# Rotated queries and keys written to DRAM by heads, in four pieces, in a two-layer hybrid decoder step

## Chip, cores and metric

The kernel runs on one core of one Trainium2 chip. The metric is the time on the device in microseconds (us), the median over several runs of one kernel. The engines are named as in the profile: PE (TensorE, matmul; PEld is its weight load), DVE (VectorE), ACT (ScalarE), POOL (GpSimd) and SP (SyncE, which here only issues DMAs). ACT issues DMAs too: the weights. The queues of SP and ACT end on the same 16 DMA engines of the core.

## What is computed

One inference step of a two-layer trunk: a prompt of 1024 positions and eight single-token samples with caches. Each layer projects its input once, runs attention on one half of the columns and an RWKV-7 recurrence on the other, and ends in a feed-forward network:

```
q, k = rope(q, pos), rope(k, pos)              # 8 heads x 64
att  = sum over patterns (128,1),(512,4),(2048,16) of softmax attention, merged by denominators
rw   = rwkv7_time_mix(token_shift(p[rwkv columns]))
x1   = layer_norm(alpha*x + concat(rms_norm(att)*gain, rw) @ w_out)
y    = layer_norm(alpha*x1 + relu(x1 @ w_ff_up)^2 @ w_ff_down)
```

The rotated keys and the values are outputs as well.

## The kernel before

**Tiling.** Activations lie transposed, 128 columns of the model on the partitions and positions along the row. The prompt is cut into two halves `h` of 512 positions (the second carries the eight sample tokens along). Every dense product is three matmuls (a high and a low part of the activation with the high part of the weight, the high part of the activation with the low part of the weight): lines 370 to 372. ACT makes the high part of a weight tile (line 343) and DVE the low part (line 344); there are four tiles of each, so PE can work on weights that were made some time before, and no further.

**Order.** PE's order is written by a planner, `Streams`: six generators (projection and feed-forward, RWKV stage 1 and 2, attention, the values' transposes, the cached keys) are interleaved by estimated times, and the result is fixed. The instructions of ACT, DVE, POOL and the DMA issues of SP are put in order at build time by a scheduler with a time model. All engines run their list in order.

**Queries and keys.** In `in_proj`, for each layer `l`, half `h` and pair of heads `p` (16 combinations), PE makes q, k and v of two heads. The columns of the weight are ordered so that a tile `t` of q or k has its 128 partitions as (f, d, r): f is the half of the rotation (2), d the head (2), r the index in it (32). `rope` (lines 657 to 664) rotates `t` with two DVE and two POOL instructions, and one DMA on SP's queue writes its 128 rows of 2 KB to `d_qkv` in DRAM (line 638). The keys go to the output too (line 640).

**Loads for the attention.** `att_load` (lines 1488 to 1531) reads them back by head. `heads` views the 128 rows as (f, d, r), so a head is two blocks of 32 rows that lie 64 rows apart. `stage` loads a head's 64 rows twice, into the upper and the lower half of a tile `stg` (line 1500, a pair of DMAs), of which there are two buffers. From each staged tile ACT makes `qS` or `kS` (lines 1522 and 1526) and POOL the low part `qL` or the low half of `kS` (lines 1523 and 1527); then the buffer is free. The first half stages q and k of two heads (four pairs), the second also the last 128 keys of the first half (six pairs), and loads `qf` and `kf` for the distant keys in two DMAs each, one per head (lines 1514 and 1515). Most loads begin at the end of the attention before (`ahead`, line 1482).

What the attention needs from this is `qS`, `qL`, `kS` for the scores `pS` (lines 1565 and 1566) and `qf`, `kf` for line 1554.

Of the kernel before, what the change touches and what calls it, by code (L numbers as in the profile page):

```python
# [28 lines left out]
HB = T // 2  # L29
# [115 lines left out]
class Streams:  # L145
# [24 lines left out]
    def note(self, *key):  # L170
        self.times[key] = self.now

    def after(self, *key, lat=0):
        return lambda: self.times[key] + lat if key in self.times else None
# [73 lines left out]
def body(ctx, tc, I, O):  # L248
    nc = tc.nc
    PE, V, A, G, S = nc.tensor, nc.vector, nc.scalar, nc.gpsimd, nc.sync  # L250
# [22 lines left out]
    def C(name):  # L273
        a, n = CAT[name]
        return cst[:, a:a + n]
# [24 lines left out]
    def both(f):  # L300
        return [[f(l, h) for h in range(2)] for l in range(DEPTH)]
# [5 lines left out]
    d_qkv = both(lambda l, h: dr.tile([4, 3, 128, HB], F32, name=f"d_qkv{l}{h}"))  # L307
# [71 lines left out]
    def dense(items, kts, xhh, xll, evac):  # L379

        res = []
        yield (0, None, 0, "d")
        yield from dense_steps(items, kts, xhh, xll, res)
        for it, p in zip(items, res):
            r = evac(it, p)
            if r is not None:
                yield r
        for i, it in enumerate(items):
            yield (res[-1] if i == 0 else 0, ("d", 900 + 500 * i), 0, None)
# [8 lines left out]
    def proj_order():  # L398
        seq = [("z", 0)]
        for p in range(4):  # L400
            if p < 3:
                seq.append(("z", p + 1))
            seq.append(("a", p))
        return seq
# [147 lines left out]
    def in_proj(l, h, hook=None, tail=None, then=None):  # L552
# [27 lines left out]
        def z_ev(p, j):  # L580
            def put(c0, n, d):
                S.dma_start(d_z[l][h][p, j, :, c0:c0 + n], d[:, :n])
            return shifted(l, h, muv(4 * j + p), 128, 4 * j + p, put)
# [30 lines left out]
        for kind, p in proj_order()[1:]:  # L614
            if kind == "a" and p == 3 and then is not None:
                yield from then()
            for j in range(3):
                w = W.take()
                if kind == "z":
                    ev = z_ev(p, j)  # L620
                    for c0, n in ck:
                        yield from dense([(w, 128, c0, n)], K8, xhc, xlc, ev)
                    continue
                seq = (2 * l + h) * 4 + p
                if j == 1 and seq > 0:
                    yield after("post", seq - 1)
                t = ap_.tile([128, HN[1]], F32, tag="qe", bufs=2, name="qe")

                def eva(it, pt):
                    _, _, c0, n = it  # L630
                    (V.tensor_copy if c0 else A.copy)(t[:, c0:c0 + n], pt[:, :n])
                for c0, n in CK[h]:
                    yield from dense([(w, 128, c0, n)], K8, xhc, xlc, eva)
                if j == 0 and h == 1:
                    t8 = ap_.tile([128, 5, 8], F32, tag="t8", name="t8")
                if j < 2:
                    rope(t, HN[h], tabs)
                    S.dma_start(d_qkv[l][h][p, j], t[:, 0:HB])
                    if j == 1:
                        S.dma_start(O["k_p"][l, p, :, h * HB:h * HB + HB], t[:, 0:HB])  # L640
                if h == 1 and j == 0:
                    if p == 0:
                        sq[l] = (rq.tile([128, 4, 32], F32, tag="q2", name="q2"), rq.tile([128, 4, 8], F32, tag="kn", name="kn"))
                        G.memset(sq[l][0], 0.0)
                    G.memset(t8[:, 1:4, :], 0.0)
                    for hd in range(2):
                        G.tensor_scalar(sq[l][0][:, p, hd:16:2], t[:, HB:HN[1]], C("hm")[:, hd:hd + 1], None, op0=ALU.mult)
                elif h == 1:
                    G.tensor_scalar(t8[:, (0, 4)[j - 1], :], t[:, HB:HN[1]], 1.0, None, op0=ALU.mult)
                    if j == 1:  # L650
                        G.tensor_scalar(sq[l][1][:, p, :], t[:, HB:HN[1]], 1.0, None, op0=ALU.mult)
            if kind == "a":
                qe[seq] = (l, h, p, t, t8 if h == 1 else None)
                note("qe", seq)
            note(kind, l, h, p)

    def rope(t, n, tabs):

        m = ap_.tile([128, HN[1]], F32, tag="rt", name="rm")
        for x in range(2):  # L660
            a, b = slice(64 * x, 64 * x + 64), slice(64 - 64 * x, 128 - 64 * x)
            V.tensor_tensor(m[a, :n], t[b, :n], tabs[b, 1, :n], op=ALU.mult)
        G.tensor_tensor(t[:, :n], t[:, :n], tabs[:, 0, :n], op=ALU.mult)
        G.tensor_tensor(t[:, :n], t[:, :n], m[:, :n], op=ALU.add)
# [179 lines left out]
    def half(l, h, prev=None):  # L844
# [169 lines left out]
        if not last:  # L1014
            store(*cl[0])
            note("proj", l + 1, h)

            def hook(i):
                if i == 0:
                    yield from ln.finish(*cl[1], spread=1)  # L1020
                ln.scale(SPI[i], evs[-1])
                if i == 5:
                    store(*cl[1])

            def tail():
                if h == 1:
                    S.dma_start(O["shift"][l + 1].rearrange("k p t -> p k t"), t[:, :, HB - 1:HN[1]])
            yield from in_proj(l + 1, h, hook, tail, mix_load(l + h, 1 - h))
        elif h == 0:
            def beside(o):  # L1030

                if o == 0:
                    yield from mixes_late[0].norm()
                if o == 1:
                    yield from ln.finish(*cl[1], spread=1)
                if o >= 1:
                    ln.scale(SPY[o], evs[-1])
            mixes_late = [mixes[l, 1]]
            yield from half(l, 1, beside)
        else:  # L1040
            yield from ln.finish(*cl[1])
# [16 lines left out]
    def dense_stream():  # L1058
        t = x_fetch(0)
        load_par()  # L1060
        x_load(0, t)
        t = x_fetch(1)
        yield from in_proj(0, 0, lambda i: init() if i == 1 else None)
        x_load(1, t)
        yield from in_proj(0, 1, then=mix_load(0, 0))
        for l, h in ((0, 0), (0, 1), (1, 0)):
            yield from half(l, h)
# [420 lines left out]
    def att_load(l, h, p):  # L1488

        qS, qL, kS = [], [], []

        def heads(src):
            return src.rearrange("(f d r) t -> d f r t", f=2, d=2)

        def stage(src, hd, n):
            t = ap_.tile([128, HB], F32, tag="stg", bufs=2, name="stg")[:, :n]
            for x in range(2):
                S.dma_start(t[64 * x:64 * x + 64], heads(src)[hd])  # L1500
            return t

        def byres(t):
            return t.rearrange("p (j a c) -> p j c a", a=32, c=4)

        def inrow(t):
            return t.rearrange("p (j c a) -> p j c a", a=32, c=4)

        qf = kf = None
        if h == 1:  # L1510
            qf, kf = (ap_.tile([128, HB], F32, tag=x, name=x) for x in ("qf", "kf"))
            for hd in range(2):
                hs = slice(64 * hd, 64 * hd + 64)
                S.dma_start(qf[hs], heads(d_qkv[l][1][p, 0])[hd])
                S.dma_start(kf[hs], heads(d_qkv[l][0][p, 1])[hd])
        for hd in range(2):
            hs, ls = slice(64 * hd, 64 * hd + 64), slice(64 - 64 * hd, 128 - 64 * hd)
            q = ap_.tile([128, HB], F32R, tag=f"q{hd}", name="qS")
            ql = ap_.tile([128, HB], F32R, tag=f"ql{hd}", name="qL")
            k = ap_.tile([128, HB + 128], F32R, tag=f"k{hd}", name="kS")  # L1520
            t = stage(d_qkv[l][h][p, 0], hd, HB)
            A.copy(inrow(q), byres(t))
            AQ.tensor_tensor(inrow(ql), byres(t), inrow(q.bitcast(F32)), op=ALU.subtract)
            for src, c, n in [(d_qkv[l][0][p, 1][:, HB - 128:HB], 0, 128)] * h + [(d_qkv[l][h][p, 1], 128 * h, HB)]:
                t = stage(src, hd, n)
                A.copy(k[:, c:c + n], t)
                AQ.tensor_tensor(k[ls, c:c + n], t[ls], k.bitcast(F32)[ls, c:c + n], op=ALU.subtract)
            qS.append(q)
            qL.append(ql)
            kS.append(k)  # L1530
        return qS, kS, qL, qf, kf, R.now + 6000 + 1000 * (h + 1)
# [328 lines left out]
```

## Time and profile before

| | us |
|---|---|
| median of three runs | 3555.35 |
| lowest and highest run | 3549.26, 3558.99 |
| the profiled execution, its own time | 3560.94 |
| its span, first to last instruction | 3559.1 |
| PE busy | 3202.7 |
| PE weight load busy | 2697.6 |
| DVE busy | 2055.5 |
| ACT busy | 1448.3 |
| POOL busy | 979.3 |

The profile shows one execution. Busy times are shares of the span; a wait is put down to what ended it. The mean granted clock of TensorE over the span is 0.949 of full speed. DMAs are issued in order on a queue; the time from issue to landing is told by who waited for the data.

### The profile page before, as it was taken

The page shows a single profiled execution, that of the slowest core. Times are in us where ns is not written, and L with a number is a line of the kernel's source. Part 1 is how long each engine was busy: PE and PEld are TensorE (multiplying, and loading weights), DVE is VectorE, ACT ScalarE, POOL GpSimd, SP SyncE. Part 2 cuts the span into 40 slices and gives each one's busy share as a digit, 9 for nine tenths or more (in the row PEclk, how much of TensorE's full clock was granted, in tenths as well). Part 3 has the DMA queues.
Part 4 walks back from the last instruction along what each step waited for, and adds up shares of the span by engine and source line. Part 5 has one row for each costly group of instructions (what it writes and reads, how often), then busy time and mean ns, then how long its engine had stood idle before and what let it go on. Part 6 is the DMA issues. An engine that isn't in the chain of part 4 may idle for free. (4 is left out here: it accounts for less than half of the span.)

```text
span 3559.1 us, 65853 instructions
## 1 busy us (share of the span) xinstructions
PE 3202.7 (90%) x24732; PEld 2697.6 (76%) x24732; DVE 2055.5 (58%) x4703; ACT 1448.3 (41%) x3266; POOL 979.3 (28%) x1841
## 2 busy tenths in 40 slices
PE   8788897977999998888999999797797999889998
PEld 6567776765777687677899998685675677789998
DVE  4455554764554664567565457465764564685556
ACT  4345333443343344344443336343443333453334
POOL 2324233531111421435211113334412121340012
PEclk9899998988999999998999999898898999999999
DMA  7334343433443335442333235344243343333332
GB/s 219 107 113 124 115 115 103 129 95 99 117 112 85 106 97 163 139 150 68 86 98 92 80 98 154 117 126 133 71 118 100 111 113 91 117 101 91 94 90 84
DMA packets 366533, 393.55 MB, mean 111 GB/s; under 512 B 141848, under 2 KB 219112, under 8 KB 366216
## 3 DMA queue, kind: packets, MB, share of 16 engines
q10 hardware_dynamic: 121152, 213.44, 20.9%
q1 hardware_dynamic: 245064, 175.92, 16.9%
q8 instruction: 195, 3.19, 0.4%
q14 instruction: 122, 1.00, 0.1%
HBM read 325.30 MB, written 63.97 MB: 109 GB/s over the span
## 5 line engine op out<-in xcount | busy, mean ns | idle before, releaser
L370 PE MATMUL dps<-xh,wh 128*128 128x256 f32 (+3 forms) x2984 | 1006.9, 337 | 31.0 <-ACT xh L758 15.0
L371 PE MATMUL dps<-xl,wh 128*128 128x256 f32 (+3 forms) x2984 | 956.8, 321 | 10.4 <-DVE xl L759 8.6
L372 PE MATMUL dps<-xh,wl 128*128 128x256 f32 (+3 forms) x2984 | 953.3, 319 | 1.2 <-DVE wl L344 1.0
L344 DVE TENSOR_TENSOR wl<-wr,wh 128x512 fp32r<-128x512 f32 (+1 forms) x772 | 581.8, 755 | 501.3 <-ACT wh L343 485.6
L343 ACT CAST wh<-wr 128x512 fp32r<-128x512 f32 (+1 forms) x772 | 475.1, 616 | 844.4 <-PE dps L371 777.8
L370 PEld LDWEIGHTS dps<-xh,wh 128*128 128x128 f32 x2984 | 576.6, 193 | 106.4 <-issue 31.0
L371 PEld LDWEIGHTS dps<-xl,wh 128*128 128x128 f32 x2984 | 576.8, 193 | 46.3 <-DVE xl L759 12.5
L372 PEld LDWEIGHTS dps<-xh,wl 128*128 128x128 f32 x2984 | 575.6, 193 | 41.0 <-DVE wl L344 2.6
L370 PE MATMUL dps<-hh,wh 128*128 128x512 f32 (+2 forms) x1600 | 536.1, 335 | 5.4 <-DVE hh L941 3.6
L371 PE MATMUL dps<-hl,wh 128*128 128x512 f32 (+2 forms) x1600 | 513.1, 321 | 4.5 <-DVE hl L830 3.3
L372 PE MATMUL dps<-hh,wl 128*128 128x512 f32 (+2 forms) x1600 | 512.0, 320 | 0.0
L370 PEld LDWEIGHTS dps<-hh,wh 128*128 128x128 f32 x1600 | 303.5, 190 | 45.2 <-issue 17.7
L371 PEld LDWEIGHTS dps<-hl,wh 128*128 128x128 f32 x1600 | 304.1, 190 | 22.6 <-DVE hl L830 4.1
L372 PEld LDWEIGHTS dps<-hh,wl 128*128 128x128 f32 x1600 | 303.9, 190 | 22.6
L1209 POOL TENSOR_TENSOR tm<-BL,XB 32x15 f32<-32x15 f32 (+7 forms) x480 | 153.0, 319 | 496.5 <-DMA BL<-d_el 375.9
L973 DVE TENSOR_TENSOR t<-dps,t 128x256 f32<-128x256 f32 (+1 forms) x240 | 123.6, 515 | 161.1 <-PE dps L372 160.7
L1211 POOL TENSOR_TENSOR XB<-XB,tm 32x15 f32<-32x15 f32 (+7 forms) x480 | 154.6, 322 | 34.4
L726 POOL TENSOR_TENSOR ln<-ln,lsq 128x256 f32<-128x256 f32 (+1 forms) x112 | 91.2, 814 | 232.5 <-ACT lsq L724 229.9
L941 DVE CAST hh<-rl 128x256 fp32r<-128x256 f32 (+2 forms) x200 | 74.4, 372 | 108.6 <-ACT rl L940 105.4
L939 ACT ACTIVATE rl<-dps 128x256 f32<-128x256 f32 (+2 forms) x200 | 88.4, 442 | 102.2 <-PE dps L372 89.9
L715 POOL TENSOR_TENSOR t<-t,ln 128x256 f32<-128x256 f32 (+1 forms) x32 | 28.1, 913 | 352.1 <-ACT ln L709 352.1
L370 PE MATMUL dps<-hh,xh 128*128 128x256 f32 (+1 forms) x368 | 112.6, 306 | 13.3 <-DVE t L1006 7.2
(345 smaller groups left out, 5098.0 us busy)
## 6 DMA issues: line engine op xcount, KB each, us to landing
wr<-in_w_ff_up ACTq DMA_DIRECT2D x272, 256.0 KB
wr<-in_w_ff_down ACTq DMA_DIRECT2D x256, 256.0 KB
wr<-in_w_in ACTq DMA_DIRECT2D x220, 256.0 KB
stg<-d_qkv SPq DMA_DIRECT2D x128, 128.0 KB
wr<-in_w_out ACTq DMA_DIRECT2D x64, 256.0 KB
z<-d_z SPq DMA_DIRECT2D x24, 384.0 KB
d_qkv<-qe SPq DMA_DIRECT2D x32, 256.0 KB
kvc<-in_cache_k SPq DMA_DIRECT2D x32, 256.0 KB
```

Source lines behind the costliest of these rows:

```text
L343: self.copies.append(A.copy(h[:, :, :m], w[:, :, :m]))
L344: V.tensor_tensor(lo[:, :, :m], w[:, :, :m], h.bitcast(F32)[:, :, :m], op=ALU.subtract)
L370: PE.matmul(p[:m, :n], wh[:, wk % 4, :m], hi, start=(i == 0), stop=False)
L371: PE.matmul(p[:m, :n], wh[:, wk % 4, :m], lo, start=False, stop=False)
L372: PE.matmul(p[:m, :n], wl[:, wk % 4, :m], hi, start=False, stop=(i == last))
L715: G.tensor_tensor(t, t, self.cm[:, c0:c0 + n], op=ALU.subtract)
L726: G.tensor_tensor(s2, s2, sq, op=ALU.add)
L939: A.activation(r, p[:, :n], AF.Relu)
L941: V.tensor_copy(hh[:, c0:c0 + n], r)
L973: V.tensor_tensor(to, p[:, :n], to, op=ALU.add)
L1209: G.tensor_tensor(tv, bc(BL[:, 17 * j + 1:17 * j + 2], [(1, m), (0, j + 1)]), bc(XB[:, 16 * j:16 * j + 1], [(0, m), (1, j + 1)]), op=ALU.mult)
L1211: G.tensor_tensor(xv, xv, tv, op=ALU.add)
```

## The change

The four blocks (f, d) of a rotated tile are written by a DMA each, to the place where head d has its 64 rows in one piece. The loads then take 64 rows that lie together, and `qf` and `kf` are one DMA each, both heads at once. Nothing else is changed: the keys' output keeps its layout.

```diff
@@ in_proj
                 if j < 2:
                     rope(t, HN[h], tabs)
-                    S.dma_start(d_qkv[l][h][p, j], t[:, 0:HB])
+                    for f in range(2):
+                        for d in range(2):
+                            a, b = 64 * f + 32 * d, 64 * d + 32 * f
+                            S.dma_start(d_qkv[l][h][p, j, b:b + 32], t[a:a + 32, 0:HB])
@@ att_load
-        def heads(src):
-            return src.rearrange("(f d r) t -> d f r t", f=2, d=2)
-
         def stage(src, hd, n):
             t = ap_.tile([128, HB], F32, tag="stg", bufs=2, name="stg")[:, :n]
             for x in range(2):
-                S.dma_start(t[64 * x:64 * x + 64], heads(src)[hd])
+                S.dma_start(t[64 * x:64 * x + 64], src[64 * hd:64 * hd + 64])
             return t
@@ att_load, second half
-            for hd in range(2):
-                hs = slice(64 * hd, 64 * hd + 64)
-                S.dma_start(qf[hs], heads(d_qkv[l][1][p, 0])[hd])
-                S.dma_start(kf[hs], heads(d_qkv[l][0][p, 1])[hd])
+            S.dma_start(qf, d_qkv[l][1][p, 0])
+            S.dma_start(kf, d_qkv[l][0][p, 1])
```

On PE the order of all instructions stays the same. On ACT, DVE and POOL no instruction is added or removed and some move by a few places. SP has 96 more writes (line 638, 32 become 128) and 16 fewer loads of `qf` and `kf`. Two places on SP's queue follow; line numbers after 641 shift by two or three in the changed kernel.

SP, the first layer's first pair of heads: the key's write, the loads of the first head's key, the second head's query and key (`stg`), and one `kf`. Before:

```order
L638 DMA d_qkv_108<-qe 128x512
L640 DMA out_k_p<-qe 128x512
L1500 DMA stg<-d_qkv_108 64x1x512 x4
L1515 DMA kf<-d_qkv_108 64x1x512
L678 DMA out_v_p<-rt 128x4x128
L680 DMA d_qkv_108<-rt 128x512
L1500 DMA stg<-d_qkv_108 64x1x512 x2
L1515 DMA kf<-d_qkv_108 64x1x512
L1471 DMA vT<-d_qkv_108 128x512
```

The same place in the changed kernel:

```order
L641 DMA d_qkv_108<-qe 32x512 x4
L643 DMA out_k_p<-qe 128x512
L1500 DMA stg<-d_qkv_108 64x512 x4
L681 DMA out_v_p<-rt 128x4x128
L683 DMA d_qkv_108<-rt 128x512
L1513 DMA kf<-d_qkv_108 128x512
L1500 DMA stg<-d_qkv_108 64x512 x2
L1474 DMA vT<-d_qkv_108 128x512
```

The write has become four, the two loads of `kf` one, which stands behind the values' write; the order is otherwise the same.

SP, second layer, second half: the loads for the second pair of heads, with `qf` and `kf`, around the sample tokens' outputs. Before:

```order
L1500 DMA stg<-d_qkv_111 64x1x512 x2
L1514 DMA qf<-d_qkv_111 64x1x512
L1515 DMA kf<-d_qkv_110 64x1x512
L1514 DMA qf<-d_qkv_111 64x1x512
L1515 DMA kf<-d_qkv_110 64x1x512
L1500 DMA stg<-d_qkv_111 64x1x512 x2
L1500 DMA stg<-d_qkv_110 64x1x128 x2
L678 DMA out_v_p<-rt 128x4x128
L680 DMA d_qkv_111<-rt 128x512
```

The same place in the changed kernel:

```order
L1500 DMA stg<-d_qkv_111 64x512 x2
L1512 DMA qf<-d_qkv_111 128x512
L1513 DMA kf<-d_qkv_110 128x512
L1500 DMA stg<-d_qkv_111 64x512 x2
L1500 DMA stg<-d_qkv_110 64x128 x2
L681 DMA out_v_p<-rt 128x4x128
L683 DMA d_qkv_111<-rt 128x512
```

Two DMAs fewer stand here between the first staged tile and the next; nothing else moved.

## Rows read from the trace of the kernel before

**Rows 1.** The page: busy time of PE and ACT, granted clock in 40 slices.
```profile
PE 3202.7 (90%) x24732; PEld 2697.6 (76%) x24732; DVE 2055.5 (58%) x4703; ACT 1448.3 (41%) x3266; POOL 979.3 (28%) x1841
...
PEclk9899998988999999998999999898898999999999
```

**Rows 2.** Busy time by stretch, 15 stretches (us) with loads for the attention.
```profile
core 0: us, PE busy (x) PEld busy (x) DVE busy (x) ACT busy (x) POOL busy (x), PEclk, DMA share, GB/s
70.00:125.00 55.00, 40.65 (x227) 31.72 (x227) 21.21 (x45) 18.23 (x40) 24.04 (x44) 0.88 0.45 134
...
2665.00:2715.00 50.00, 30.40 (x193) 20.77 (x189) 16.80 (x44) 12.29 (x25) 8.42 (x14) 0.76 0.25 76
sum 860.00, PE 599.93 PEld 486.99 DVE 393.15 ACT 313.25 POOL 309.99; mean PE 40.00 PEld 32.47 DVE 26.21 ACT 20.88 POOL 20.67
```

**Rows 3.** The same view, five stretches with attention and RWKV steps, but without such loads.
```profile
190.00:230.00 40.00, 40.00 (x288) 28.97 (x286) 25.54 (x72) 16.53 (x45) 15.29 (x40) 1.00 0.40 115
...
2575.00:2665.00 90.00, 89.43 (x772) 66.78 (x768) 54.98 (x147) 41.85 (x102) 13.59 (x42) 1.00 0.43 122
sum 380.00, PE 376.31 PEld 300.22 DVE 242.48 ACT 167.87 POOL 110.45; mean PE 75.26 PEld 60.04 DVE 48.50 ACT 33.57 POOL 22.09
```

**Rows 4.** Who waited for whom, whole span: us in total, times, longest us.
```profile
DVE wl L344 <- ACT wh L343: 485.6, 309, 17.3
...
ACT kS L1526 <- DMA stg<-d_qkv: 191.7, 33, 16.6
...
ACT qS L1522 <- DMA stg<-d_qkv: 120.7, 19, 15.3
```

**Rows 5.** Instructions in order of time, one load: start, us, what, [idle before <-releaser].
```profile
2393.24 11.96 SPq L1500 DMA_DIRECT2D stg<-d_qkv  x4
...
2396.01 0.60 ACT L343 CAST wh<-wr 128x512 fp32r<-128x512 f32 x1
2397.37 0.33 ACTq L342 DMA_DIRECT2D wr<-in_w_out  x1
2411.87 1.09 ACT L1522 CAST qS<-stg 128x512 fp32r<-128x512 f32 x1 [15.25 <-DMA stg<-d_qkv]
...
2413.68 0.75 ACT L1325 COPY TV<-pPQ 64x256 f32<-64x256 f32 x2
...
2414.10 1.12 PE L1342 MATMUL pO<-LB,TV 128*64 128x128 f32 x8 [14.16 <-ACT TV L1325]
```

**Rows 6.** Busy time by stretch: one in which hardly any other DMA runs beside a stage.
```profile
2553.00:2559.00 6.00, 6.00 (x36) 5.77 (x37) 6.00 (x5) 0.00 (x0) 5.18 (x9) 0.76 0.13 46
```

**Rows 7.** DMA issues: how many, KB each.
```profile
stg<-d_qkv SPq DMA_DIRECT2D x128, 128.0 KB
...
kf<-d_qkv SPq DMA_DIRECT2D x16, 128.0 KB
```

**Rows 8.** The chain that ended last, pieces that end on a stage: start, us, what.
```profile
2241.29 12.67 DMA stg<-d_qkv
...
2396.64 15.15 DMA stg<-d_qkv
...
2698.09 7.96 DMA stg<-d_qkv
```

**Rows 9.** The same chain: other DMAs from issue to landing.
```profile
2236.54 3.04 DMA d_qkv<-qe
...
2855.60 2.18 DMA d_el<-LB
...
2893.37 3.29 DMA ST<-in_state_wkv
```

**Rows 10.** In order of time: the state's load in two halves of 64 partitions, and its user.
```profile
2892.83 1.14 SPq L1656 DMA_DIRECT2D ST<-in_state_wkv  x2
...
2896.78 0.69 DVE L1657 TENSOR_TENSOR dt<-ST,DV 128x512 f32<-128x512 f32 x1 [2.99 <-DMA ST<-in_state_wkv]
```

**Rows 11.** Busy time by stretch: 33 stretches at half clock among those of rows 2.
```profile
88.10:94.90 6.80, 4.92 (x14) 4.05 (x15) 4.22 (x9) 2.12 (x6) 2.77 (x7) 0.50 0.34 114
105.10:108.60 3.50, 2.84 (x9) 2.48 (x10) 1.18 (x4) 0.00 (x0) 2.25 (x7) 0.51 0.63 188
...
sum 290.40, PE 151.15 PEld 125.36 DVE 101.94 ACT 98.21 POOL 99.36; mean PE 4.58 PEld 3.80 DVE 3.09 ACT 2.98 POOL 3.01
```

**Rows 12.** By tile: issues and casts, times each: ns min/median/max, first and last start.
```profile
L1500 SPq DMA_DIRECT2D stg<-d_qkv x160: 482/509/3642, 75.5 to 2698.1; - x160
L638 SPq DMA_DIRECT2D d_qkv<-qe x32: 319/332/2788, 73.4 to 2430.7; - x32
...
L1522 ACT CAST qS<-stg x32: 1087/1111/1131, 84.1 to 2694.8; 128x512 fp32r<-128x512 f32 x32
L1523 POOL TENSOR_TENSOR qL<-stg,qS x32: 1510/1526/1702, 85.2 to 2696.0; 128x512 fp32r<-128x512 f32 x32
```

## Prediction

> **What bounds the kernel now.** I read the page first: PE is busy for 90% of the span and the granted clock dips below full in many slices [rows 1]. So the question is where PE stands still. The busy time by stretch answers it. In 15 stretches of 860 us in all, those in which the attention's operands are loaded, PE works for 599.93 us: 260 us of idle time, at granted clocks down to 0.75 [rows 2]. In five stretches of 380 us with the same attention and RWKV steps but without such loads, PE works for 376.31 us, 1% idle, at full clock [rows 3]. The whole span has 3559.1 - 3202.7 = 356 us of idle time; nearly three quarters of it lies beside these loads.
>
> The waits tell who is late: ACT stood 191.7 us before `kS` casts and 120.7 us before `qS` casts until a stage landed [rows 4]. ACT works in order, and behind these casts stand the casts of the weights: DVE's longest waits are for them, 17.3 us in one case [rows 4]. The order of time shows one such case whole [rows 5]. SP issues four stage DMAs in 11.96 us, ACT waits 15.25 us for one of the tiles, what stands behind the cast on ACT (a copy that PE needs, line 1325) is late, and PE is idle for 14.16 us although everything else it needed was there. The last weight cast before it began at 2396.01.
>
> Why is a stage late? While hardly anything else is on its way, the mean busy share of the 16 DMA engines is 0.13 at 46 GB/s [rows 6]. 0.13 x 16 = 2.1: a stage moves on two engines. From its second issue to landing a pair of 256 KB takes 7.96 us, and 12.67 and 15.15 us where others queue before it [rows 8]. There are 128 stage DMAs of 128 KB, 32 of 32 KB, and 32 for `qf` and `kf` of 128 KB [rows 7, 12], 22 MB in all; at 46 GB/s that is 478 us of two engines, most of the 860 us.
>
> The two engines fit the shape of the access: its outermost extent is f, of two. The Trainium skill ("DMA: Bandwidth & Descriptors", "Why a DMA increments its semaphore by 16 and not by 1") says that a DMA runs on the largest number of engines up to 16 that divides the outermost extents of both sides; by that rule it is 2 before and 16 after, and a pair's transfer alone would fall to an eighth. The row at 0.13 agrees for before; no row shows the new load itself.
>
> **Part 1, the loads.** The nearest row to the new pair is the decode state, loaded by two DMAs of 64 partitions and 2 KB each, 128 KB apiece, the same bytes into the same partitions: 3.29 us from second issue to landing [rows 9], 3.95 us from first issue to the DVE instruction that uses it (2892.83 to 2896.78) [rows 10]. I take it for the new pair, against 7.96 us [rows 8]. The queueing that makes 12 to 15 us of it goes with the two engines.
>
> What stays: a stage buffer is free only when POOL is done with it, so each of the 16 loads should still show about one wait of a landing's length, 16 x 3.95 = 63 us, and the work itself idles at 1% of the 600 us it takes, 6 us. So of 260 us 69 stay, and **191 us** go. The ends: 254 us (260 - 6, no wait shows, PE has buffered work for each) and 153 us (the idle time falls only as a lone pair does, by (7.96 - 3.29) / 7.96 = 59%).
>
> **Part 2, the clock.** After the gaps the clock is granted at 0.50, the 1.2 GHz level: 33 stretches of 290 us within those of rows 2, in which PE is busy for 151.15 us [rows 11]. At 2.4 GHz that work would take half, so 75.6 us are lost. If this falls as the idle time does (69 of 260 left, 27%), **55 us** come back. The ends: 75 us, and 47 us if each of 16 remaining waits still costs a stretch of 3.5 us, the shorter of the two stretches shown [rows 11] (16 x 3.5 / 2 = 28 lost).
>
> **Part 3, the writes.** 96 DMAs more on SP at 0.332 us each [rows 12], 32 us of SP in all. Per tensor the fourth piece is issued 3 x 0.332 = 1.0 us later, the third, which a first head needs, 0.66 us. SP is not short of time: its four stage issues that took 11.96 us [rows 5] need four times 0.509 [rows 12], so far more than the new issues cost is spent on a queue that is backed up. 16 loads of `qf` and `kf` fall away. Behind the four pieces on SP stand the keys' output and the next stage; nobody else waits. Where the load follows the write at once (about half of the 16 loads; the others begin at the end of the attention before, when the data lies there long since) the delay shows: 8 x 0.66 = **5 us lost**. The ends: nothing, and 32 us (1.0 us for each of 32 tensors). What hides the rest is PE's buffered work; in a load that runs late it would show whole.
>
> Here a rule of the skill speaks against the change. A write of 256 KB lands in 3.04 us and a pair of 64 KB DMAs in 2.18 us [rows 9]: small ones land hardly sooner. The Trainium skill (same page, "Rules for kernel authors") says to coalesce small transfers, since under 64 KB one pays mostly overhead; a 256 KB write cut into 64 KB pieces would by it pay the overhead four times. That row of 2.18 us is for two in flight together, so I take the overhead as shared, and the serial case as a rival.
>
> **Part 4, what moves.** PE's order is the same. ACT's casts stand within a few places of where they stood, so a stage that lands early is used where the order has it, not before: `qS` on ACT takes 1.1 us and `qL` on POOL 1.5 us [rows 12] as before. I cost this at nothing; the cover is PE's buffered weights.
>
> **Sum.** 191 + 55 - 5 = 241 us. The profiled execution took 3560.94 us by its own time, so 3320 us; the median of the runs is 5.6 us lower: **3314 us**.
>
> **The rivals.** *Two buffers become the bound.* A round of a q and a k stage is landing, ACT cast, POOL: 3.95 + 1.11 + 1.53 = 6.6 us, three rounds in the second half and two in the first, some 13 to 20 us per load. If PE's buffered work covers about half of that and 7 us show in each, 112 us stay: 260 - 6 - 112 = 142, with the clock at 55% of 75.6 (41), less 5: 178 us gained, 3377 us. For it: POOL's share of the wait doesn't change. Against it: the first two stages of most loads are fetched early, and in rows 5 PE kept working for about 6 us after the preceding cast.
>
> *The pieces land one after the other.* 4 x 2.18 = 8.72 instead of 3.04 us, 5.7 us later for the two tensors of the 8 loads that follow at once: 91 us given back, 3405 us; the gain would still be there. Against it: the pair in rows 10 is two DMAs in one landing time.
>
> *The change doesn't do what it says, and is slower.* If the number of engines isn't set by the shape of the access, and a stage still runs at 46 GB/s, only the later writes are left: up to 32 us on the path, 3555 + 32 = 3587 us, and 3560 if 5 show. It decides where the DMA share beside a lone stage is still 0.13. Against it: the state's load, of the same bytes and partitions, lands in 3.29 us.
>
> **How the numbers follow.** Forecast 0.80, two buffers 0.12, serial pieces 0.04, no spreading 0.04. The ends of the parts give 254 + 75 = 329 us (3226 us at the median) and 153 + 47 - 32 = 168 us (3387 us). The low end takes every bound at once, so I stop at 3240; the high end takes in both smaller gains: 3430. A measurement of this kernel tells about 0.3% (11 us) from no change. Faster by more: the first three, 0.96; the last is split, 0.02 the same and 0.02 slower.
>
> **What would show it.** Right: a pair of stages lands in 3 to 4 us; ACT's waits on a stage fall from 312 us to under 100; idle time of PE in the load stretches falls below 100 us; the clock's dips go with it; SP's issues of a stage no longer take microseconds. The first rival shows as waits of SP on POOL with short landings, the second as a write that lands 6 us late. I am wrong if the loads land early and PE's idle time in these places stays, held by someone else.

## The result, and the profile after

The changed kernel takes 3294.07 us (median of four runs, 3284.82 to 3297.23) where the kernel before takes 3555.17 (four runs, 3549.26 to 3558.99): a ratio of 0.9263, interval 0.924 to 0.9285. 241 us less were forecast and 261 came; the time lies 20 us under the forecast, inside the range.

The profiled execution took 3297.23 us by its own time. First the page: span, busy time, granted clock in 40 slices.

```profile
span 3295.4 us, 65986 instructions
...
PE 3148.5 (96%) x24732; PEld 2656.9 (81%) x24732; DVE 2065.4 (63%) x4703; ACT 1449.2 (44%) x3266; POOL 985.1 (30%) x1841
...
PEclk9999999999999999999999999999999999999999
```

PE does the same 24732 matmuls in 54.2 us less (3202.7 before [rows 1]): the dips of the clock are nearly gone. Its idle time, span less busy time, falls from 356.4 to 146.9 us, by 209.5. Span is busy time and idle time, so the two make up the 263.7 us by which it is shorter; where on the span they fell, the next view tells.

Next the stretches with loads for the attention, chosen in the same way as those of [rows 2]: 15 again, but 593 us long and not 860. The first, the last and the sum:

```profile
70.00:105.00 35.00, 32.25 (x186) 25.37 (x185) 20.86 (x42) 17.29 (x38) 23.32 (x43) 1.00 0.73 202
...
2427.00:2450.00 23.00, 23.00 (x155) 15.43 (x154) 13.58 (x37) 12.39 (x24) 7.33 (x9) 1.00 0.47 136
sum 593.00, PE 546.92 PEld 447.29 DVE 402.56 ACT 312.68 POOL 316.36; mean PE 36.46 PEld 29.82 DVE 26.84 ACT 20.85 POOL 21.09
```

PE is idle in them for 593.00 - 546.92 = 46 us (260 before). Outside them it is idle for 101 us (96 before). So the idle time fell beside the loads and nowhere else. In the first and in the last stretch the clock is granted in full (0.88 and 0.76 before [rows 2]); the lowest of the 15 is 0.85.

Who waited for whom, over the whole span:

```profile
DVE wl L344 <- ACT wh L343: 334.3, 303, 5.0
...
ACT kS L1524 <- DMA stg<-d_qkv: 38.9, 21, 4.7
...
ACT qS L1520 <- DMA stg<-d_qkv: 11.7, 9, 2.9
```

The two casts of staged tiles are lines 1524 and 1520 now. ACT stands 38.9 us before `kS` (191.7 before [rows 4]) and 11.7 before `qS` (120.7), 50.6 us in 30 waits (312.4 in 52). The longest such wait is 4.7 us, not 16.6, and DVE's longest wait for a weight's high part 5.0, not 17.3. The view of the tile `d_qkv` has the issues (ns min/median/max):

```profile
L1500 SPq DMA_DIRECT2D stg<-d_qkv x160: 444/547/1472, 75.6 to 2439.5; - x160
L641 SPq DMA_DIRECT2D d_qkv<-qe x128: 302/421/1433, 72.2 to 2207.7; - x128
```

Compare [rows 12]: the median issue of a stage is no shorter (0.547 us, 0.509 before), but the longest took 3.642 us and takes 1.472. A write of 32 rows takes SP 0.421 us, one of 128 rows took 0.332.

Now the load of [rows 5] again, in order of time:

```profile
2182.98 1.11 SPq L1500 DMA_DIRECT2D stg<-d_qkv  x2
2184.19 0.54 SPq L1512 DMA_DIRECT2D qf<-d_qkv  x1
2184.78 0.42 SPq L1513 DMA_DIRECT2D kf<-d_qkv  x1
2185.29 4.20 SPq L1500 DMA_DIRECT2D stg<-d_qkv  x4
...
2186.39 0.62 ACT L1524 CAST kS<-stg 128x512 fp32r<-128x512 f32 x1 [1.69 <-DMA stg<-d_qkv]
```

The pair is issued from 2182.98 and cast at 2186.39: 3.41 us from first issue to use, with `qf` and `kf` right behind it. The next four stage DMAs leave SP in 4.20 us where four took 11.96. The chain that ended last has one piece left that ends on a stage, where the one before has ten, and some 20 us earlier a write:

```profile
2173.04 1.78 DMA d_qkv<-qe
...
2193.57 2.66 DMA stg<-d_qkv
```

Stages stood in that chain with up to 15.15 us [rows 8]; the write takes 1.78 us from the last of its four issues, where the whole one took 3.04 from its only one [rows 9]. SP began the first of the four at 2171.58, so from first issue to landing it is 3.24 us: in pieces a tensor lands no sooner, and hardly later.

### The profile page after: what moved, and what is told of

It reads as the page before. It is cut to its first block, busy times and chain, and to the rows that moved or that the text cites. A ratio compares the mean times of both kernels' runs of the same rounds, so it can differ in the third digit from the quotient of the medians.

```text
span 3295.4 us, 65986 instructions
## 1 busy us (share of the span) xinstructions
PE 3148.5 (96%) x24732; PEld 2656.9 (81%) x24732; DVE 2065.4 (63%) x4703; ACT 1449.2 (44%) x3266; POOL 985.1 (30%) x1841
## 5 line engine op out<-in xcount | busy, mean ns | idle before, releaser
L370 PE MATMUL dps<-xh,wh 128*128 128x256 f32 (+3 forms) x2984 | 991.9, 332 | 18.6 <-ACT wh L343 8.1
L371 PE MATMUL dps<-xl,wh 128*128 128x256 f32 (+3 forms) x2984 | 945.5, 317 | 7.8 <-DVE xl L762 6.3
L344 DVE TENSOR_TENSOR wl<-wr,wh 128x512 fp32r<-128x512 f32 (+1 forms) x772 | 578.1, 750 | 348.6 <-ACT wh L343 334.3
L370 PEld LDWEIGHTS dps<-xh,wh 128*128 128x128 f32 x2984 | 566.1, 190 | 90.8 <-issue 26.7
L371 PEld LDWEIGHTS dps<-xl,wh 128*128 128x128 f32 x2984 | 566.9, 190 | 42.3 <-DVE xl L762 9.8
L372 PEld LDWEIGHTS dps<-xh,wl 128*128 128x128 f32 x2984 | 566.3, 190 | 40.5 <-DVE wl L344 3.9
```

Of the source, the lines that this page charges most:

```text
L344: V.tensor_tensor(lo[:, :, :m], w[:, :, :m], h.bitcast(F32)[:, :, :m], op=ALU.subtract)
L370: PE.matmul(p[:m, :n], wh[:, wk % 4, :m], hi, start=(i == 0), stop=False)
L371: PE.matmul(p[:m, :n], wh[:, wk % 4, :m], lo, start=False, stop=False)
L372: PE.matmul(p[:m, :n], wl[:, wk % 4, :m], hi, start=False, stop=(i == last))
```

## The experiments

My theory was that of the prediction: a load was late because it ran on two of 16 engines, and it ran on two because the outermost extent of its access is two. The rivals: what helps is that rows lie together in DRAM, or that the writes or the fewer loads of `qf` and `kf` matter, or that the landing is not what PE waits for, but the order of ACT. The experiments ran on chips on which the kernel before takes 3567 to 3570 us, so they are compared by their ratios to it.

In the table PE's idle time is span less busy time, and the waits are those of the two casts' engine on staged tiles (ACT, in the last two rows POOL), of one profiled execution each. The kernel before has 356.4 us of idle time, 312.4 us of waits and a clock of 0.949.

| kernel | ratio and interval | PE idle, us | waits, us | clock |
|---|---|---|---|---|
| changed | 0.9263 (0.924 to 0.9285) | 146.9 | 50.6 | 0.983 |
| e1_rows_outermost | 0.925 (0.9235 to 0.9266) | 154.4 | 70.8 | 0.985 |
| e2_two_outermost | 0.9806 (0.9792 to 0.9821) | 276.5 | 256.9 | 0.953 |
| e3_four_outermost | 0.9427 (0.9413 to 0.9441) | 187.0 | 136.6 | 0.974 |
| e4_eight_outermost | 0.9303 (0.9289 to 0.9318) | 154.4 | 87.7 | 0.980 |
| e5_stages_only | 0.9422 (0.9404 to 0.9441) | 196.5 | 135.3 | 0.973 |
| e6_far_only | 0.9815 (0.9797 to 0.9833) | 291.2 | 259.0 | 0.953 |
| e7_eight_pieces | 0.9275 (0.9259 to 0.9291) | 152.6 | 56.1 | 0.981 |
| e8_two_writes | 0.9585 (0.9571 to 0.96) | 234.7 | 105.8 | 0.964 |
| e9_casts_on_pool | 1.0018 (1.0009 to 1.0028) | 369.6 | 229.5 | 0.948 |
| e10_after_casts_on_pool | 0.935 (0.9336 to 0.9364) | 170.5 | 57.6 | 0.975 |

**The order of the dimensions alone.** The kernel before, with its one write of 128 rows and its blocks 64 rows apart; only the order in which a load walks over them differs, the 32 rows outside and the two blocks inside. The 64 rows of a head then lie in another order on the partitions, for queries and keys alike, and a score sums over them.

```diff
         def heads(src):
-            return src.rearrange("(f d r) t -> d f r t", f=2, d=2)
+            return src.rearrange("(f d r) t -> d r f t", f=2, d=2)
```

> The layout and the single write of the kernel before; only the loads name their rows in another order, r outermost and f inside (extents 32, 2, 512 instead of 2, 32, 512). The 64 rows of a head still lie in two blocks, and neighbours in the tile now come from places 128 KB apart. Queries and keys get the same order of rows, so the scores are the same sums. Theory 'engines' (the outermost extent of the access sets on how many DMA engines a load runs): the stages spread over 16 engines as in the changed kernel, ACT's waits on a stage fall from 312 to some 50 us, 3285 us (3270 to 3305), perhaps a few us below the changed kernel, since 96 writes are spared. Theory 'blocks' (what counts is that a head's rows lie together): nothing gained, 3555 us or more.

Measured: 3298.96 us, 0.925. That is the whole gain, with rows that do not lie together, without the 96 writes more and with the 32 loads of `qf` and `kf`. From the waits, and from the tile's view:

```profile
ACT kS L1526 <- DMA stg<-d_qkv: 56.3, 24, 5.9
```

```profile
L1500 SPq DMA_DIRECT2D stg<-d_qkv x160: 507/591/1705, 75.8 to 2440.9; - x160
...
L638 SPq DMA_DIRECT2D d_qkv<-qe x32: 319/330/974, 73.8 to 2205.4; - x32
```

That rows lie together in DRAM is not what helps. The two ways can't be told apart in time: their intervals overlap, and the difference, 0.0013, is under the 0.3% that a measurement of this kernel tells.

**The other way round: rows together, but walked over as two, four or eight outermost.** The changed kernel, its stages alone; `qf`, `kf` and the writes stay as changed.

```diff
-                S.dma_start(t[64 * x:64 * x + 64], src[64 * hd:64 * hd + 64])
+                S.dma_start(t[64 * x:64 * x + 64], src[64 * hd:64 * hd + 64].rearrange("(r f) t -> f r t", f=2))
```

The other two have `f=4` and `f=8`.

> The changed kernel with its four writes, its layout and its single loads of qf and kf; only the stages take the 64 rows, which lie together, as two interleaved sets of 32 (extents 2, 32, 512). 'Engines': the stages run on two engines again, a lone stage at a DMA share of 0.13; all of the gain is lost but what qf and kf gave (32 of 192 transfers, about a sixth): 3500 us (3450 to 3560). 'Blocks': a head's 128 KB are still one piece, so the gain stays: 3295 us.

> As the run with two sets, but four sets of 16 rows (extents 4, 16, 512). 'Engines': four engines, a pair's 256 KB take half as long (about 3.7 us and a landing's fixed part); most of the loads' queueing goes: 3350 us (3310 to 3420). 'Blocks': 3295 us.

> As before with eight sets of eight rows (extents 8, 8, 512). 'Engines': eight engines, a pair's transfer is a quarter of the two engines' 7 us; within 30 us of the changed kernel: 3305 us (3290 to 3330). 'Blocks': 3295 us.

Measured: 3499.26, 3362.17 and 3316.77 us. The waits of ACT for a stage, with two, with four and with eight outermost:

```profile
ACT kS L1524 <- DMA stg<-d_qkv: 151.2, 33, 8.3
...
ACT qS L1520 <- DMA stg<-d_qkv: 105.7, 20, 8.3
```

```profile
ACT kS L1524 <- DMA stg<-d_qkv: 87.3, 28, 6.1
...
ACT qS L1520 <- DMA stg<-d_qkv: 49.3, 20, 5.2
```

```profile
ACT kS L1524 <- DMA stg<-d_qkv: 60.5, 26, 5.2
...
ACT qS L1520 <- DMA stg<-d_qkv: 27.2, 16, 4.3
```

In sum 257, 137 and 88 us, and 50.6 in the changed kernel with 64 rows outermost; the longest wait goes 8.3, 6.1, 5.2, 4.7 us. The same 128 KB, in one piece in DRAM, are slow when they are named as two times 32 rows: the chain of the kernel with two has, among others,

```profile
2482.92 11.41 DMA stg<-d_qkv
...
2636.82 7.29 DMA stg<-d_qkv
```

where 12.67 to 15.15 and 7.96 us stood in [rows 8]. The last pair of the last load is the same 256 KB in every kernel, and little else is on its way beside it. The chains have it, from its second issue to landing, with 7.29 us for two (above), and for four and for eight with

```profile
2505.10 4.21 DMA stg<-d_qkv
```

```profile
2459.26 3.44 DMA stg<-d_qkv
```

(3.49 in the first experiment). The busy time by stretch, in a quiet part of that transfer, with two, four and eight, has the mean share of the 16 DMA engines and GB/s as its last two numbers:

```profile
2642.00:2643.50 1.50, 1.16 (x3) 0.34 (x2) 0.00 (x0) 0.00 (x0) 0.00 (x0) 0.50 0.13 49
```

```profile
2506.50:2508.50 2.00, 2.00 (x13) 1.64 (x11) 1.21 (x4) 0.00 (x0) 0.00 (x0) 1.00 0.26 97
```

```profile
2460.00:2461.50 1.50, 1.50 (x10) 0.88 (x9) 1.50 (x4) 0.00 (x0) 0.00 (x0) 1.00 0.49 158
```

Times 16 these shares are 2.1, 4.2 and 7.8 engines. So what counts is the outermost extent, and what it sets is the number of engines. The sets are interleaved, each of every second, fourth or eighth row; the wider step has the shorter time, so the step is not the reason. The gain per doubling falls (137 us, 45 us, and by the ratios 0.0040 of 3567, 14 us to the changed kernel), as it must when a part of the landing stays: 256 KB at 49, 97 and 158 GB/s are 5.4, 2.7 and 1.7 us, and 1.5 to 1.9 us of each landing are left. The rule of the Trainium skill that the prediction named ("DMA: Bandwidth & Descriptors", "Why a DMA increments its semaphore by 16 and not by 1") would give 2, 4, 8 and 16 engines here; the shares agree for the first three. For 16 no stretch has a stage alone, and the time agrees.

**Which loads.** The kernel before, with the row order of the first experiment in the stages alone, or in `qf` and `kf` alone. A helper `rows`, and then either line:

```diff
+        def rows(src):
+            return src.rearrange("(f d r) t -> d r f t", f=2, d=2)
...
-                S.dma_start(t[64 * x:64 * x + 64], heads(src)[hd])
+                S.dma_start(t[64 * x:64 * x + 64], rows(src)[hd])
...
-                S.dma_start(qf[hs], heads(d_qkv[l][1][p, 0])[hd])
-                S.dma_start(kf[hs], heads(d_qkv[l][0][p, 1])[hd])
+                S.dma_start(qf[hs], rows(d_qkv[l][1][p, 0])[hd])
+                S.dma_start(kf[hs], rows(d_qkv[l][0][p, 1])[hd])
```

> The kernel before, with its layout and write; the stages name their rows with r outermost (32, 2, 512), qf and kf keep their loads with f outermost. 'Engines': only qf and kf are left on two engines (32 transfers of 128 KB, 4.2 MB, 91 us of the two engines at 46 GB/s, all in the second halves, where the stages queue behind them): 3335 us (3305 to 3385), ratio 0.927 to 0.949. If the gain of the whole change came from qf and kf: no change.

> The other part alone: qf and kf with r outermost, the stages as before. 'Engines': the same as the changed kernel with its stages on two engines, ratio 0.981 (0.972 to 0.990), since the writes cost next to nothing; that and the part with the stages alone should make more together than the whole gain's 7.5% only if both wait on the same two engines: 2% here, 5 to 7% there.

Measured: 3364.4 us, 0.9422, and 3501.54 us, 0.9815. The gains are 5.8% and 1.9%; their sum is 7.6%, and both at once gave 7.5%. They add up. The loads of `qf` and `kf` bring a quarter, though the view of these tiles before puts down only 2.1 us of waiting for them: they were issued between stages on SP's queue, and made the stages late: with them alone changed, ACT's waits on stages fall from 312.4 to 259.0 us. The kernel with two outermost in its stages (0.9806) is nearly the same case as the second of these, with four writes in place of one and with rows that lie together: the four writes cost nothing that can be measured there either.

**Eight pieces.** The changed kernel with twice the writes, 16 rows each: if pieces land one after the other, this shows it twice.

```diff
-                            a, b = 64 * f + 32 * d, 64 * d + 32 * f
-                            S.dma_start(d_qkv[l][h][p, j, b:b + 32], t[a:a + 32, 0:HB])
+                            for g in range(2):
+                                a, b = 64 * f + 32 * d + 16 * g, 64 * d + 32 * f + 16 * g
+                                S.dma_start(d_qkv[l][h][p, j, b:b + 16], t[a:a + 16, 0:HB])
```

> The changed kernel with eight pieces of 16 rows in place of four of 32: 128 writes more at 0.42 us (the median issue in the changed kernel), 1.7 us later for the last piece of a tensor. 'Hidden by PE's buffered work': within 0.4% of the changed kernel, ratio 0.926 to 0.931. 'Pieces pay one after the other' (2.18 us each, four more per tensor, 8.7 us for each of the 16 tensors that are loaded at once): 140 us more, ratio 0.965.

Measured: 3310.74 us, 0.9275, not to be told from the changed kernel; landing one after the other should have cost 140 us. Pieces do not land one after the other.

**Two writes.** The changed kernel with two writes of 64 rows in place of four of 32. On the side of DRAM each has two blocks outermost, so by the theory it runs on two engines.

```diff
                     for f in range(2):
-                        for d in range(2):
-                            a, b = 64 * f + 32 * d, 64 * d + 32 * f
-                            S.dma_start(d_qkv[l][h][p, j, b:b + 32], t[a:a + 32, 0:HB])
+                        S.dma_start(d_qkv[l][h][p, j].rearrange("(d f r) t -> f d r t", d=2, f=2)[f], t[64 * f:64 * f + 64, 0:HB])
```

> The changed kernel with two writes in place of four, one per f, whose place in DRAM has the head outermost (extents 2, 32, 512): half the issues, but, if the rule holds for writes as for loads, each on two engines. 'Engines': a tensor's 256 KB land after some 8 us instead of 3, 5 us later for 16 tensors that are loaded at once, and loads queue behind: 3345 us (3310 to 3400), ratio 0.931 to 0.955. 'Fewer writes are cheaper': ratio 0.923 to 0.926.

Measured: 3421.45 us, 0.9585: the direction was right and the size was not; it lies above the range that I had given. The waits tell what I had left out:

```profile
ACT kS L1522 <- DMA stg<-d_qkv: 72.7, 21, 10.0
...
ACT qe L631 <- DMA d_qkv<-qe: 46.7, 7, 10.7
...
ACT qS L1518 <- DMA stg<-d_qkv: 33.1, 12, 9.6
```

Besides the loads that wait for a late write (ACT's waits on stages 105.8 us, 50.6 in the changed kernel), the write holds the tile `qe` that it reads. There are two of these, so ACT's copy of the next projection into `qe` waits for the landing: 46.7 us, 6.2 in the changed kernel. In order of time on ACT, with the start of the wait:

```profile
2281.88 0.42 ACT L1396 ACTIVATE gq<-gq 128x256 f32<-128x256 f32 x1
2290.54 0.37 ACT L631 COPY qe<-dps 128x256 f32<-128x256 f32 x1 [8.24 <-DMA d_qkv<-qe]
```

The chain has this write with 8.90 us, and in the quiet part of it the share is that of two engines for a write too:

```profile
2284.50:2287.00 2.50, 2.50 (x46) 2.29 (x45) 2.43 (x3) 0.00 (x0) 2.33 (x4) 1.00 0.13 44
```

PE is idle for 88 us more than in the changed kernel; ACT waits 55 us more for stages and 40 us more for `qe`, which is of that size. What is issued behind such a pair on SP's queue is late as well: the chain has `d_el<-LB`, issued right behind one, with 8.58 us, where 2.18 stood [rows 9]. So it matters that a write is cut in such a way that each piece is one block on both sides: two writes with two blocks each cost 3.2% of the time, four and eight with one block cost nothing that can be measured.

**Is it ACT's order?** The prediction's way from a late stage to an idle PE goes over ACT, which works in order. Here the two casts are done by POOL, in the kernel before and in the changed one; the loads stay as they are.

```diff
-            A.copy(inrow(q), byres(t))
+            G.tensor_scalar(inrow(q), byres(t), 1.0, None, op0=ALU.mult)
...
-                A.copy(k[:, c:c + n], t)
+                G.tensor_scalar(k[:, c:c + n], t, 1.0, None, op0=ALU.mult)
```

> The kernel before, loads on two engines as they were; only the casts of the staged tiles to qS and kS are made by POOL instead of ACT, so that ACT never waits for a stage. 'Through ACT's order' (PE stood still because the weights' casts and the copies it needs stood behind a stage's cast on ACT): ACT's waits on stages go, POOL's grow by as much; PE is held only where the scores themselves or POOL's own work (the rotation, RWKV's triangular blocks) come late: 3420 us (3350 to 3500), ratio 0.94 to 0.98. 'Through the queue' (PE stood still because other loads and writes queued behind the stages on the two engines): no change, ratio 0.99 to 1.01.

> The changed kernel with the same casts on POOL. ACT still waits 52 us on stages in the changed kernel; PE is idle for 147 us of which some 30 lie beside loads. 'Through ACT's order': what is left of it goes, 10 to 20 us gained if POOL has the time (it is busy for 30%), ratio 0.921 to 0.926; if POOL's rotation and triangular blocks come late in turn, 10 to 30 us lost, ratio 0.929 to 0.935.

Measured: 3575.03 us, 1.0018, and 3336.32 us, 0.935. I had expected the first to be 2 to 6% faster than before; it is not faster at all. The waits of that kernel:

```profile
DVE wl L344 <- ACT wh L343: 354.8, 300, 10.9
...
POOL kS L1526 <- DMA stg<-d_qkv: 153.0, 24, 18.5
...
POOL qS L1522 <- DMA stg<-d_qkv: 76.5, 16, 11.1
...
PE pT L1280 <- DMA X<-d_el: 38.0, 11, 15.7
...
PE pS L1565 <- POOL kS L1527: 31.9, 4, 19.6
```

No instruction of ACT reads a stage any more, and DVE's wait for the high parts of the weights, which is the way over ACT, falls from 485.6 [rows 4] to 354.8 us, near the 334.3 of the changed kernel. (The view still puts 75 us of ACT's waits down to a stage's landing, at instructions that read none; what they waited for is not settled.) But POOL waits in ACT's place, 229.5 us, and PE for other things. Summed over the lines of the view, PE's waits for ACT fall from 162.3 to 93.6 us; those for POOL rise from 12.5 to 47.8 (for `kS` up to 19.6 at once), and those for the tiles `X` of the RWKV steps, which come by way of `d_el`, from 4.0 to 38.0. PE's idle time stays (369.6 us). So the way over ACT was there, but taking it away gains nothing while the landing stays late.

In one place the queue on SP is seen to hold PE without ACT or POOL between:

```profile
2392.32 12.51 SPq L1500 DMA_DIRECT2D stg<-d_qkv  x4
...
2407.41 2.51 SPq L680 DMA_DIRECT2D d_qkv<-rt  x1
...
2417.74 1.40 DVE L662 TENSOR_TENSOR rm<-qe,tab 64x520 f32<-64x520 f32 x2 [19.48 <-DMA d_qkv<-rt]
...
2421.26 0.69 PE L1356 MATMUL pO<-FG,Zp 64*64 64x128 f32 x4 [15.25 <-DVE FG L1347]
```

The values' write stands behind four stages; `rm` takes the buffer of the tile `rt` that this write reads, so DVE waits 19.48 us for it, and PE 15.25 us for what stands behind `rm` on DVE. The kernel before has one such wait too (15.5 us), the changed one none. How much of the rest is POOL's order and how much the queue stays open; POOL's casts are also slower (`qS` 1.99 us by their median, 1.11 on ACT [rows 12]). In the changed kernel the same move loses some 31 us (0.935 to 0.9263, of 3569), at the end of the second of the two ranges that I had given (46 us of PE's idle time lie beside its loads, not the 30 written there): ACT is the better place for the casts either way.

More buffers for `stg` were not tried.

## Why the prediction was right, point by point

**The cause** was right, and it is shown both ways round: the same loads with another order of dimensions have the gain without the change, and rows in one piece lose it when they are named as two. The DMA share beside a lone pair (0.13, 0.26 and 0.49) goes with the outermost extent. The gain goes over both of ACT's waits and PE's clock, as described. That ACT's order is *the* carrier, as the first part has it, is too strong: with the casts on POOL the idle time stays and others wait, in one place for the queue on SP itself.

**Part 1, the loads**: 191 us forecast; with the 5 that part 3 takes back 186, and 209.5 measured. The landing was taken from the state's load as 3.95 us and is 3.41 in the load shown. The term that was mis-sized is "each of the 16 loads should still show about one wait of a landing's length, 16 x 3.95 = 63 us". ACT does wait for a sum of that order, 50.6 us, but in 30 waits, none longer than 4.7; PE, which has weights made ahead, is idle for 46 us in these stretches for whatever reason, and not the 74 that were left by the forecast of both parts; outside them it is idle for 5 us more. A wait of ACT was set equal to idle time of PE. That PE's stock of weights covers short ones in part is the likely reason; no run separates it from the shorter landing.

**Part 2, the clock**: 55 us forecast, 54.2 measured as PE's busy time. That it fits to 1 us is in part luck: the forecast let the loss fall as the idle time does, and with 46 of 260 us left, not 69, that rule gives 62.

**Part 3, the writes**: 5 us lost forecast. Neither the 96 writes fewer of the first experiment nor the 128 more of the one with eight pieces gives a difference that can be told from nothing, so the true price lies near the low end of the range; 5 us are too few for a measurement to confirm or refute. The issue itself was priced too low, 0.332 us against 0.421.

**Part 4, what moves**: nothing was forecast, and outside the load stretches PE is idle for 101 us against 96, so nothing of size moved there.

The sum was 241 us and the span fell by 263.7. The difference of 23 us is in the idle time (186 forecast, 209.5 measured), the clock's term being right to 1 us in its result; whether up to 5 of it belong to the price of the writes is not settled.

**The rivals.** *Two buffers become the bound* had 112 us of idle time left beside the loads; there are 46. SP does wait on POOL before a stage, but less than before (64.2 us there, then line 1523):

```profile
SPq L1500 <- POOL qL L1521: 47.5, 19, 11.5
```

*Pieces one after the other* falls with the eight pieces and with the write, whose four pieces take 3.24 us from the first issue and not 8.72. *The change doesn't do what it says* falls with the time itself. The sign named for it, the share beside a lone stage, can't be read in the changed kernel, since a weight's load runs beside the stages of its last load:

```profile
2437.40:2441.00 3.60, 3.60 (x19) 2.57 (x17) 2.12 (x4) 1.22 (x4) 1.56 (x1) 1.00 0.42 133
```

The shares with four and eight outermost, 0.26 and 0.49, take its place. Its idea came nearest to being true in the two writes above: had the change been made so, the loads would have got their engines and the writes lost theirs.

Of the signs, those of the landing (3 to 4 us), ACT's waits (under 100), the idle time (under 100) and the clock came as told. "SP's issues of a stage no longer take microseconds" holds for the longest ones alone; the median issue didn't fall.

## What to carry to other kernels

Where the mean busy share of the DMA engines beside a lone transfer is far below one, read its access pattern: here the outermost extent set how many engines it got (a share of 0.13 with two, 0.26 with four), for loads and (0.13 with two) for a write, so a small block index belongs inside the rows, not outside. One edit of the order of dimensions was worth as much as the change with its 96 writes, so where the order of the rows in the tile is free, as here, try that before moving data. And a slow write makes others wait: who loads what it wrote, who needs the tile that it reads, and what stands behind it on the queue.

## What the runs showed of the hardware

- For these loads it counts in which order the rows are named, not whether they lie together: 64 adjacent rows of 2 KB, 128 KB in one piece, named as two interleaved sets of 32, land as late as two blocks that lie 64 rows apart (7.29 and 7.96 us for a pair), and such blocks with the rows named outermost land in 3.49 us.
- A lone pair of loads shows a mean DMA share of 0.13 at 46 to 49 GB/s with two outermost, 0.26 at 97 with four and 0.49 at 158 with eight: some 20 to 24 GB/s for each engine used. A write with two outermost on the side of DRAM shows 0.13 as well.
- Cutting a write of 256 KB into four of 64 KB or eight of 32 KB cost nothing that can be measured. The Trainium skill ("DMA: Bandwidth & Descriptors", "Rules for kernel authors") says to coalesce because below 64 KB one pays mostly overhead; here, where the pieces are in flight together, the runs do not show it, for pieces of 32 KB neither.
- SP's time to issue a DMA did not fall with its size: the writes of 32 partitions take 0.421 us by their median, those of 128 took 0.332, and the issue of a stage did not get shorter when its landing did (0.547 and 0.509).
